# State space stage: decay operands of three groups in four as one VectorE product over four heads, of the fourth as four ScalarE activations

## The chip, the cores and the metric

The kernel runs on one core of a Trainium2 chip. The metric is device time in microseconds (us). Engines are named as in the profile: PE is TensorE (PEld its weight loads), DVE is VectorE, ACT is ScalarE, POOL is GpSimd, SP the engine that issues the DMAs.

## The reference, cut to what matters

Two layers of a hybrid block over 1024 latent tokens and 256 context tokens, model width 1024. Each layer has one input projection, three groups of heads side by side (neighbourhood attention, differential attention, a bidirectional state space model), an output projection, and a gated MLP with a convolution. The change touches one product in the state space part. With la = dt * a per token and head, and chunks of 128 tokens, the reference computes

```
cs = jnp.cumsum(la, axis=-1)
lmat = jnp.exp(jnp.where(lower, cs[..., :, None] - cs[..., None, :], -jnp.inf))
cb = jnp.einsum('bcign,bcjgn->bgcij', cm, bm)
y_diag = jnp.einsum('bgcij,bgecij,bcjgep->bcigep', cb, lmat, xdt)
```

for 8 heads in 2 groups of 4, once forwards and once backwards in time. All of it is float32.

## The kernel before, in words

The 1280 tokens are 10 chunks of 128: 8 of latents, 2 of context. Layer 0 produces all 10, layer 1 only the 8 of the latents, so there are 18 chunks in all.

In `ssd_out` the decay matrix of a group of four heads (`decay(g)`, lines 987 to 1004) comes from a matmul: a triangular 0/1 matrix `tri` times an operand `mf` of 128 partitions by 4 heads by 128 columns. `mf` holds, for each of four heads, a triangular 0/1 mask (`C(C_PI)` forwards, `C(C_SI)` backwards, 128x128 in SBUF) times a value per partition, `lah[:, e, c, h]`. `lah` holds la in two parts, e = 0 the rounded high part and e = 1 the rest. So a group needs four tiles `mf` (two directions, two parts), numbered i = 0 to 3 in the code, and four matmuls (line 998) that add up in one PSUM tile `pd` of the tag "s" (2 buffers). The tag "mf" has 3 buffers. ACT then takes the exponential into a tile `M` (line 1001, through the helper `act`, whose line is 93), and DVE multiplies it by the two masked score tiles `cbu` and `cbl` (line 1003). `out_pair(g)` uses `M` in the matmuls of line 1018.

Before the change, each `mf` is written by four products of 128x128, heads 0 and 2 on GpSimd, heads 1 and 3 on VectorE (line 996). This makes 18 chunks x 2 groups x 4 tiles = 144 tiles, and 576 products, half on each engine.

`ssd_all` steps the chunks as a generator. It runs in the background of the projections of the same layer: `dfproj` (differential q, k and v) and `naqk` (neighbourhood q and k). After each projection chunk `bg_step` advances the generator at 1.2 steps (`SR`). A projection chunk is 24 matmuls into a PSUM tile of the tag "mm" (3 buffers) and then an evacuation: square on ACT, a matmul for the mean, four activations on ACT and two or three products on DVE (`rstd`, lines 406 to 414), the scaling on DVE (lines 493 and 690), for differential q and k a rotation with one product on GpSimd (line 497), and a split into two parts (lines 281 and 282, or 697 and 698 with the rest on GpSimd). In the same chunk loop GpSimd also writes `xd` (964), `yo` (985) and `y` (1048) of the state space part and `wL` (269), the low part of the next projection weights.

The program is written as a data flow; a planner orders the instructions of each engine from estimated times, and adds the semaphores. Each engine then works through its own list in order, so an instruction that waits holds all behind it on its engine. GpSimd and ACT issue no DMAs here; all are issued on SP.

Of the kernel before, what the change touches and what calls it, by code (L numbers as in the profile page):

```python
# [12 lines left out]
ACTF = mybir.ActivationFunctionType  # L13
ALU = mybir.AluOpType
# [66 lines left out]
def hybrid_kernel(ctx, tc, xin, cc, w_ada, bada, gmf, w_in, w_dt, w_out, w_up, w_dn, vec, cst, rope, nab, out):  # L81
    nc = tc.nc
    V, S, G, PE, SP = nc.vector, nc.scalar, nc.gpsimd, nc.tensor, nc.sync
# [8 lines left out]
    def act(**kw):  # L92
        ins = S.activation(**kw)  # L93
        f = kw["func"]
        if f == ACTF.Silu:
            last_silu[0] = ins
            if last_exp[0] is not None:
                tc.add_manual_dep(ins.ins, last_exp[0].ins.name, nosync, reason="table")
        elif f in (ACTF.Exp, ACTF.Ln) and anchor[0] is not None:
            tc.add_manual_dep(ins.ins, anchor[0].ins.name, nosync, reason="table")  # L100
            cur_exp[0] = ins
        return ins
# [77 lines left out]
    def C(off, n=128, p=128):  # L180
        return cs[0:p, off:off + n]
# [93 lines left out]
    def pst(tag, bufs):  # L275
        if mmx[0] is None:
            tag, bufs = "B", 4
        return psx[1].tile([128, 512], F32, tag=tag, name=tag, bufs=bufs)
# [664 lines left out]
    def ssd_out(l, p, c, dts, lah, ecs):  # L943
        def v4(a):
            return a.rearrange("p (h d) -> p h d", h=4)
# [24 lines left out]
        for nm, mk in (("cbu", C_PI), ("cbl", C_SI)):  # L970
            t = p.tile([128, 2, 128], F32, tag=nm, name=nm, bufs=1)
            V.tensor_tensor(out=t, in0=pcb[:, 0:256].rearrange("p (g i) -> p g i", g=2),
                            in1=C(mk).unsqueeze(1).to_broadcast([128, 2, 128]), op=ALU.mult)
# [14 lines left out]
        def decay(g):  # L988
            pd = pst("s", 2)
            i = 0  # L990
            for d, mk in ((0, C_PI), (1, C_SI)):
                for e in range(2):
                    mf = p.tile([128, 4, 128], F32R, tag="mf", name="mf", bufs=3)
                    for hh in range(4):
                        h = 8 * d + 4 * g + hh
                        (V if hh % 2 else G).tensor_scalar(out=mf[:, hh], in0=C(mk), scalar1=lah[:, e, c, h:h + 1], scalar2=1.0,  # L996
                                        op0=ALU.mult, op1=ALU.mult)
                    PE.matmul(pd, tri[:, d], mf.rearrange("p h i -> p (h i)"), start=(i == 0), stop=(i == 3))  # L998
                    i += 1
            mm_ = p.tile([128, 2, 4, 128], F32, tag="M", name="M", bufs=2)  # L1000
            act(out=mm_[:, 1], in_=v4(pd), func=ACTF.Exp)
            for d in range(2):
                V.tensor_tensor(out=mm_[:, d], in0=mm_[:, 1],
                                in1=cbm[d][:, g].unsqueeze(1).to_broadcast([128, 4, 128]), op=ALU.mult)
            Ms[g] = mm_
# [3 lines left out]
        def out_pair(g):  # L1009
            if g == 0:  # L1010
                py[0] = pst("o", 1)
            for q in (2 * g, 2 * g + 1):
                PE.matmul(py[0][:, q * 128:(q + 1) * 128], offs[0][:, q * 128:(q + 1) * 128], ident,
                          start=True, stop=False)
                for d in range(2):
                    for e in range(2):
                        h = 2 * q + e
                        PE.matmul(py[0][64 * e:64 * e + 64, q * 128:(q + 1) * 128], xd[d][:, h * 64:(h + 1) * 64],
                                  Ms[g][:, d, h % 4], start=False, stop=(d == 1))

        decay(0)
        yield
        decay(1)
        yield
        out_pair(0)
# [6 lines left out]
        for q in range(4):  # L1032
            V.scalar_tensor_tensor(out=y[:, q], in0=ux[:, q], scalar=vcol(l, V_DSK + q),
                                   in1=py[:, q * 128:(q + 1) * 128], op0=ALU.mult, op1=ALU.add)
# [8 lines left out]
        for q in range(4):  # L1043
            V.scalar_tensor_tensor(out=y[:, q], in0=y[:, q], scalar=vcol(l, V_SN + q), in1=rs,
                                   op0=ALU.mult, op1=ALU.mult)
# [836 lines left out]
```

## Time and profile before

| | |
|---|---|
| median of 3 timed runs | 3596.09 us (3594.19 to 3603.89) |
| the profiled execution, own time | 3589.41 us |
| its span, first to last instruction | 3587.6 us |
| mean granted clock of TensorE | 0.965 |
| busy: PE, PEld | 3284.6 us (92%), 2582.9 us (72%) |
| busy: DVE, ACT, POOL | 2350.0 us (66%), 1515.8 us (42%), 1766.9 us (49%) |

Busy times are sums over the whole span, and matmul ends are modelled, so a busy PE isn't PE at its peak. The state space output runs twice: from about 310 to 580 us (layer 0) and from about 2215 to 2430 us (layer 1). These are the stretches that the views below are asked for. In a row of grouped instructions, "128x512 fp32r<-128x128 f32" gives the shapes written and read, "x160" the count, then the busy time in us, the mean of one in ns, and behind the second bar the idle time of the engine just before them with what ended it.

### The profile page before, as it was taken

The page shows a single profiled execution, that of the slowest core. Times are in us where ns is not written, and L with a number is a line of the kernel's source. Part 1 is how long each engine was busy: PE and PEld are TensorE (multiplying, and loading weights), DVE is VectorE, ACT ScalarE, POOL GpSimd, SP SyncE. Part 2 cuts the span into 40 slices and gives each one's busy share as a digit, 9 for nine tenths or more (in the row PEclk, how much of TensorE's full clock was granted, in tenths as well). Part 3 has the DMA queues.
Part 4 walks back from the last instruction along what each step waited for, and adds up shares of the span by engine and source line. Part 5 has one row for each costly group of instructions (what it writes and reads, how often), then busy time and mean ns, then how long its engine had stood idle before and what let it go on. Part 6 is the DMA issues. An engine that isn't in the chain of part 4 may idle for free. (4 is left out here: it accounts for less than half of the span.)

```text
span 3587.6 us, 50299 instructions
## 1 busy us (share of the span) xinstructions
PE 3284.6 (92%) x17970; PEld 2582.9 (72%) x17970; DVE 2350.0 (66%) x4208; ACT 1515.8 (42%) x2641; POOL 1766.9 (49%) x1319
## 2 busy tenths in 40 slices
PE   6998998899897999999998998998999969999899
PEld 3876776666676888887787776776666757777677
DVE  6635876778475655556858754985884576676763
ACT  4233434677353233233335523344774443333343
POOL 2136663656335444444554226763664445555444
PEclk8999999999998999999999999998999989999999
DMA  8255444753731222225443246446655522223643
GB/s 294 102 195 172 130 127 137 188 150 98 248 110 62 93 73 85 95 85 183 144 137 104 81 135 206 133 124 176 184 151 181 184 68 84 96 91 97 235 121 120
DMA packets 328474, 491.24 MB, mean 137 GB/s; under 512 B 28320, under 2 KB 182048, under 8 KB 327968
## 3 DMA queue, kind: packets, MB, share of 16 engines
q1 hardware_dynamic: 328224, 488.03, 42.6%
q8 instruction: 142, 2.33, 0.3%
q14 instruction: 108, 0.88, 0.1%
HBM read 349.25 MB, written 138.67 MB: 136 GB/s over the span
## 5 line engine op out<-in xcount | busy, mean ns | idle before, releaser
L269 POOL TENSOR_TENSOR wL<-wr,wH 128x1024 fp32r<-128x1024 f32 x80 | 203.8, 2551 | 417.1 <-ACT wH L268 389.5
L1227 POOL TENSOR_TENSOR wL<-wr,wH 128x1024 fp32r<-128x1024 f32 (+1 forms) x102 | 228.6, 2243 | 339.0 <-ACT wH L1224 304.4
L1227 POOL TENSOR_TENSOR wL<-wd,wH 128x512 fp32r<-128x512 f32 (+1 forms) x134 | 214.0, 1616 | 206.0 <-ACT wH L1224 201.4
L1227 POOL TENSOR_TENSOR wL<-ws,wH 128x512 fp32r<-128x512 f32 x168 | 253.4, 1528 | 112.0 <-ACT wH L1224 111.9
L758 DVE TENSOR_SCALAR_CACHE_REDUCE e<-s 128x512 f32<-128x512 f32 (+1 forms) x400 | 228.7, 588 | 105.5 <-PE s L757 101.0
L1227 DVE TENSOR_TENSOR bL<-br,bH 128x512 fp32r<-128x512 f32 x154 | 144.8, 943 | 133.9 <-ACT bH L1224 133.0
L93 ACT ACTIVATE e<-e,nm 128x1280 f32<-128x1280 f32 (+1 forms) x144 | 183.0, 1271 | 52.4 <-DVE nm L761 47.5
L757 PE MATMUL s<-ks,qst 128*128 128x512 f32 (+1 forms) x400 | 165.3, 450 | 39.5 <-DVE e L758 25.7
L1224 ACT CAST wH<-wr 128x1024 fp32r<-128x1024 f32 (+1 forms) x102 | 91.8, 905 | 252.4 <-PE mm L1219 188.2
L1224 ACT CAST wH<-ws 128x512 fp32r<-128x512 f32 x168 | 98.0, 619 | 231.5 <-PE mm L1219 94.3
L776 POOL TENSOR_TENSOR e<-e 128x1280 f32<-128x1280 f32 (+1 forms) x72 | 192.9, 2679 | 3.9
L774 POOL TENSOR_SCALAR e<-e,rho 128x1280 f32<-128x1280 f32 (+1 forms) x72 | 89.6, 1245 | 179.4 <-DVE rho L766 77.1
L996 POOL TENSOR_SCALAR mf<-cs,lah 128x128 fp32r<-128x128 f32 x288 | 141.3, 507 | 48.1 <-PE s L998 46.3
L1374 DVE SCALAR_TENSOR_TENSOR fa<-fpad,vc,fa 128x1282 f32<-128x1282 f32 (+1 forms) x88 | 140.6, 1653 | 36.7 <-ACT fa L93 36.7
L1224 ACT CAST bH<-br 128x512 fp32r<-128x512 f32 x154 | 95.3, 620 | 137.8 <-DMA br<-hdd 67.4
L1219 PE MATMUL A<-bL,wH 128*128 128x512 f32 x352 | 141.7, 403 | 11.9 <-DVE bL L1227 11.7
L1224 ACT CAST wH<-wd 128x512 fp32r<-128x512 f32 (+1 forms) x134 | 86.7, 682 | 136.0 <-PE B L1219 70.9
L422 PE MATMUL mm<-h_0H,wH 128*128 128x512 f32 x320 | 134.1, 420 | 4.4 <-DVE aqs L690 3.1
L1220 PE MATMUL A<-bH,wL 128*128 128x512 f32 x352 | 138.0, 398 | 0.0
L757 PEld LDWEIGHTS s<-ks,qst 128*128 128x128 f32 x400 | 75.4, 201 | 84.9 <-DVE e L758 52.6
L422 PE MATMUL mm<-h_1H,wH 128*128 128x512 f32 x320 | 132.2, 414 | 1.5 <-ACT z L93 1.5
L423 PE MATMUL mm<-h_0L,wH 128*128 128x512 f32 x320 | 131.1, 410 | 2.3 <-DVE h_0L L402 2.3
(871 smaller groups left out, 10812.8 us busy)
## 6 DMA issues: line engine op xcount, KB each, us to landing
wr<-in_w_up_dram SPq DMA_DIRECT2D x94, 512.0 KB
br<-hdd SPq DMA_DIRECT2D x154, 256.0 KB
wa<-in_w_ada_dram SPq DMA_DIRECT2D x56, 512.0 KB
wr<-in_w_in_dram SPq DMA_DIRECT2D x48, 512.0 KB
hdd<-c SPq DMA_DIRECT2D x88, 256.0 KB
wr<-in_w_ada_dram SPq DMA_DIRECT2D x40, 512.0 KB
wd<-in_w_dn_dram SPq DMA_DIRECT2D x38, 512.0 KB
hdd<-fa SPq DMA_DIRECT2D x66, 256.0 KB
```

What stands on the lines that cost most here:

```text
L93: ins = S.activation(**kw)
L269: (eng or G).tensor_tensor(out=wl, in0=wr, in1=wh.bitcast(F32), op=ALU.subtract)
L422: PE.matmul(ps[:, :n], wh[:, ks], r, start=(i == 0), stop=False)
L757: PE.matmul(s_, qst[b, qt][:, mi], ks[b][:, mi, k0 + c:k0 + c + n], start=True, stop=True)
L758: V.tensor_scalar(out=e[:, c:c + n], in0=s_, scalar1=1.0, scalar2=None, op0=ALU.mult, op1=ALU.max, accum_out=mx[:, ci:ci + 1])
L776: G.tensor_tensor(out=es[0][:, 0:nk], in0=es[0][:, 0:nk], in1=es[1][:, 0:nk], op=ALU.add)
L996: (V if hh % 2 else G).tensor_scalar(out=mf[:, hh], in0=C(mk), scalar1=lah[:, e, c, h:h + 1], scalar2=1.0, op0=ALU.mult, op1=ALU.mult)
L1219: PE.matmul(ps, wh, bl, start=False, stop=False, skip_group_check=True)
L1220: PE.matmul(ps, wl, bh, start=False, stop=last, skip_group_check=True)
L1224: S.copy(out=out_h, in_=src)
L1227: le.tensor_tensor(out=out_l, in0=src, in1=out_h.bitcast(F32), op=ALU.subtract)
L1374: V.scalar_tensor_tensor(out=a[:, :W], in0=pads[r][:, j:j + W], scalar=vcol(l, fw + j), in1=a[:, :W], op0=ALU.mult, op1=ALU.add)
```

## The change

In `decay(g)`, the four products of a tile become one VectorE product over 128 x 4 x 128 for i = 0, 1, 2: the mask is broadcast over the heads and the four values per partition over the columns. For i = 3 (backwards, low part) they become four ScalarE activations of function Identity with the value as the scale. GpSimd writes no part of `mf` any more. Tiles, buffers, matmuls and all else stay.

```
                     mf = p.tile([128, 4, 128], F32R, tag="mf", name="mf", bufs=3)
-                    for hh in range(4):
-                        h = 8 * d + 4 * g + hh
-                        (V if hh % 2 else G).tensor_scalar(out=mf[:, hh], in0=C(mk), scalar1=lah[:, e, c, h:h + 1], scalar2=1.0,
-                                        op0=ALU.mult, op1=ALU.mult)
+                    h0 = 8 * d + 4 * g
+                    if i == 3:
+                        for hh in range(4):
+                            act(out=mf[:, hh], in_=C(mk), func=ACTF.Identity, scale=lah[:, e, c, h0 + hh:h0 + hh + 1])
+                    else:
+                        V.tensor_tensor(out=mf, in0=C(mk).unsqueeze(1).to_broadcast([128, 4, 128]),
+                                        in1=lah[:, e, c, h0:h0 + 4].unsqueeze(2).to_broadcast([128, 4, 128]), op=ALU.mult)
                     PE.matmul(pd, tri[:, d], mf.rearrange("p h i -> p (h i)"), start=(i == 0), stop=(i == 3))
```

## Rows read from the trace of the kernel before

**Rows 1.** Busy time of each engine in the two stretches, with granted clock

```profile
310.00:580.00 270.00, 247.34 (x1428) 188.77 (x1426) 221.38 (x455) 105.52 (x211) 168.84 (x223) 0.97 0.42 130
2215.00:2430.00 215.00, 203.32 (x1152) 155.51 (x1150) 175.51 (x351) 85.56 (x166) 147.38 (x188) 0.96 0.46 143
sum 485.00, PE 450.66 PEld 344.28 DVE 396.89 ACT 191.07 POOL 316.22; mean PE 225.33 PEld 172.14 DVE 198.44 ACT 95.54 POOL 158.11
```

**Rows 2.** Waits of PE in 310 to 580: us in total, times, longest

```profile
PE s L1040 <- DVE yrs L1039: 3.1, 4, 1.5
PE s L998 <- DVE mf L996: 3.1, 2, 1.9
PE mm L422 <- DVE aqs L690: 3.1, 2, 2.9
PE mm L422 <- DVE qn L493: 2.1, 1, 2.1
PE o L1018 <- DVE M L1003: 1.9, 2, 1.7
PE s L998 <- POOL mf L996: 1.1, 3, 0.6
```

**Rows 3.** The same view, 2215 to 2430

```profile
PE t L496 <- DVE qn L493: 6.4, 2, 5.9
PE o L1018 <- DVE M L1003: 2.2, 1, 2.2
PE o L1013 <- POOL yo L985: 1.0, 2, 0.7
PE s L998 <- POOL mf L996: 0.9, 3, 0.4
```

**Rows 4.** Tile mf: min/median/max ns; and "who waited for it (us, times)"

```profile
L996 POOL TENSOR_SCALAR mf<-cs,lah x288: 363/442/1316, 310.9 to 2423.1; 128x128 fp32r<-128x128 f32 x144
L996 DVE TENSOR_SCALAR mf<-cs,lah x288: 267/314/2430, 313.8 to 2423.1; 128x128 fp32r<-128x128 f32 x144
...
  POOL mf L996: 47.9, 32
  DVE mf L996: 18.0, 16
```

**Rows 5.** Busy time of the instructions on tile mf alone: PE, PEld, DVE, POOL

```profile
sum 485.00, PE 52.40 PEld 25.63 DVE 110.86 POOL 141.33; mean PE 26.20 PEld 12.81 DVE 55.43 POOL 70.67
```

**Rows 6.** Line 1003, a DVE product of 512 columns from two SBUF tiles, all 72

```profile
L1003 DVE TENSOR_TENSOR M<-M,cbu x36: 675/700/2517, 335.9 to 2427.7; 128x512 f32<-128x512 f32 x36
L1003 DVE TENSOR_TENSOR M<-M,cbl x36: 674/692/2776, 339.1 to 2428.9; 128x512 f32<-128x512 f32 x36
```

**Rows 7.** The same products grouped, 310 to 580

```profile
L1003 DVE TENSOR_TENSOR M<-M,cbu 128x512 f32<-128x512 f32 x20 | 17.7, 885 | 3.4 <-ACT M L93 3.3
L1003 DVE TENSOR_TENSOR M<-M,cbl 128x512 f32<-128x512 f32 x20 | 16.8, 838 | 0.3
```

**Rows 8.** The same, 2215 to 2430

```profile
L1003 DVE TENSOR_TENSOR M<-M,cbl 128x512 f32<-128x512 f32 x16 | 15.5, 967 | 0.2
L1003 DVE TENSOR_TENSOR M<-M,cbu 128x512 f32<-128x512 f32 x16 | 13.3, 829 | 0.8 <-ACT M L93 0.7
```

**Rows 9.** In order of time: four DVE products in a row, eight on POOL

```profile
439.86 0.93 DVE L996 TENSOR_SCALAR mf<-cs,lah 128x128 fp32r<-128x128 f32 x4
...
374.61 4.06 POOL L996 TENSOR_SCALAR mf<-cs,lah 128x128 fp32r<-128x128 f32 x8
```

**Rows 10.** ACT, activations of 128x128 in 310 to 580

```profile
L93 ACT ACTIVATE yrv<-s,epst 128x128 f32<-128x128 f32 x9 | 3.2, 361 | 1.2 <-PE s L1040 1.1
L93 ACT ACTIVATE yrs<-yrs 128x128 f32<-128x128 f32 x9 | 2.8, 307 | 0.1
```

**Rows 11.** Waits of ACT in 310 to 580

```profile
ACT qoh L93 <- PE t L491: 31.3, 10, 9.5
ACT zt L93 <- DVE y L1035: 16.5, 7, 5.4
ACT dfv L511 <- PE mm L448: 12.8, 6, 4.6
```

## The prediction

> **What bounds the kernel now.** I read the busy table by stage first, over the two stretches in which the state space output runs [rows 1]. PE is busy 450.7 of 485 us, so it sets the pace, with 34.3 us of idle time. DVE is next: 396.9 us, 82% of the time. POOL has 316.2 us (65%) and ACT 191.1 us (39%). The reader should see that two engines are nearly full in the same stretch. PE's idle time can't be waste alone, because an 82% busy DVE that works in order is late whenever its work comes in bunches. The granted clock is 0.97 and 0.96, so PE lost another 0.03 x 270 + 0.04 x 215 = 16.7 us of full-speed work there. Idle time and lost clock, 51 us, are the most that anything done here can give back.
>
> Next I asked what ended PE's waits [rows 2, 3]. Those that a DVE or POOL result ended add up to 14.4 us in layer 0 and 10.5 us in layer 1, 24.9 us together. Of these 3.1 + 1.1 + 0.9 = 5.1 us are for the decay operand itself (DVE once, POOL twice); the other 19.8 us are for other results of the two engines (the projection's scaling, M, the norm).
>
> Then the tile mf [rows 4, 5]. Its 576 products keep DVE busy for 110.9 us and POOL for 141.3 us of the two stretches: more than a quarter of all DVE work there, and 45% of POOL's. The writers also wait for one of the three buffers to be read by its matmul: POOL 47.9 us in 32 waits, DVE 18.0 us in 16. Waiting means that all behind them on the same engine waits too.
>
> **The change part by part.** Removed on POOL: 288 products, 141.3 us [rows 5], and the buffer waits of 47.9 us. POOL falls from 316 to 175 us. Nothing of it was PE's bound directly except the 2.0 us of POOL mf waits [rows 2, 3], but eight of these products take 4.06 us in a row [rows 9], and they were the slower half of every tile.
>
> Removed on DVE: 288 products of 128 columns, 110.9 us, a mean of 385 ns where four in a row take 0.93 us, 233 ns each [rows 5, 9]. So DVE paid more than half as much again as the operation costs undisturbed, while both engines worked on the same tile.
>
> Added on DVE: 108 products of 512 columns. The trace has no product with both operands broadcast; the nearest row is line 1003, also 512 columns, two SBUF inputs, one of them broadcast. It takes 675 ns at least and 700 in the median [rows 6], and 829 to 967 ns in the mean [rows 7, 8]; over all 72, 63.3 us / 72 = 879 ns. Bounds for the 108: 108 x 0.675 = 72.9 us and 108 x 0.967 = 104.4 us, so DVE saves between 38 and 6 us. The mean lies over the median because a few take up to 2.8 us; POOL was 65% busy while they ran, and will be 36% busy. I take 0.79 us, half-way between median and mean: 85.3 us, a saving of 25.6 us. The same relief should reach the other DVE products with two SBUF inputs. For line 1003 the excess over 0.69 us is 63.3 - 49.7 = 13.6 us; I take half of it, 7 us, and nothing for the other lines (bounds 0 and 13.6). DVE: 396.9 - 25.6 - 7 = 364 us, 75% in place of 82%.
>
> One rule speaks against this edit. The trace has the old product at 233 ns per 128 columns and the nearest new one at 700 ns per 512, so one long product is cheaper than four short ones by 0.23 us [rows 6, 9]. The Trainium skill, "VectorE: DVE Perf Modes", section "The perf-mode tier table", says that float32 tensor_scalar reaches twice the rate and tensor_tensor only the single rate: per column the new form is the slower one. By that rate alone 512 columns would take 2 x 0.93 = 1.86 us, and the 108 products 201 us instead of 85; the median of 700 ns does not agree with reading the rule so, since most of a short product is a fixed cost, and the row decides.
>
> Added on ACT: 36 tiles x 4 = 144 activations of 128x128. Rows for this size are 307 ns (SBUF input) and 361 ns (PSUM input, a bias tile) [rows 10]; a scale read per partition isn't among those with 128 columns, so I take the range: 44 to 52 us, 48 us in the middle. ACT rises from 191 to 239 us of 485, 49%. Identity is used in the same stretches already, so no new function. What hides it: ACT mostly waits for others. In layer 0 it waits 31.3 us for the mean's matmul, 12.8 us for the value projection and 16.5 us for a DVE product [rows 11]. So its own work costs nothing as long as it is free when the projection's evacuation arrives.
>
> Moved to ACT with it: the buffer wait. With three buffers, the tile i = 3 takes the buffer of i = 0 of the same group and must wait for that tile's matmul. Today such a wait costs POOL 47.9 / 32 = 1.5 us and DVE 1.1 us. On ACT, the exponential of the group before and the activations of the projection's evacuation are queued behind it; DVE's scaling (lines 493 and 690) waits for those, and PE's next projection chunk waits for the PSUM tile. Bounds: nothing, if the order puts the four activations behind the matmul, or 36 x 1.5 = 54 us of held ACT. I take nothing net on PE, since ACT waits for PE more than PE for ACT; both ends stay in the range. The DMA issues aren't touched: no DMA is issued on ACT or POOL, and SP passes nothing.
>
> The sum. For the operand itself: the last product of a group of four tiles no longer comes from a POOL run of 4 us but from three DVE products (3 x 0.7 = 2.1 us) beside 4 x 0.33 = 1.3 us on ACT. Of 5.1 us I expect 1 to be left: -4. For the other 19.8 us: how late a nearly full engine is goes roughly with busy / idle, 0.82 / 0.18 = 4.5 before and 0.75 / 0.25 = 3.0 after, a third less: -6.6. For the clock: it fell around PE's pauses, so I take the same third of 16.7: -5.6. Together -16 us. Against the profiled execution (3589.4 us, of which 1.8 us lie outside the span) this gives 3573 us; the median of the timed runs is 6.7 us above that execution, so the forecast on the median is 3596 - 16 = 3580 us.
>
> **The rivals.**
>
> A: PE takes nothing of it. PE is 93% busy in the stretches, and what DVE no longer delays is delayed by something else: a transfer, a PSUM tile, ACT. For: 34.3 us idle are only partly ended by DVE and POOL. Against: 24.9 of them are. What is left then is the direct operand waits, at most -5: 3591 us.
>
> B: slower, by ACT as the new place of the wait. Mechanism: the four activations of i = 3 stand ahead of an evacuation in ACT's list and wait for the matmul of i = 0. Price: 36 waits x 1.5 us = 54 us, against the 16 us of the forecast. It is slower by more than 0.3% (11 us) from the point where 27 of the 54 us, half, reach PE; with three quarters, 40 us, it comes to 3596 + 24 = 3620 us. For: the buffer waits are in the trace now, 48 in number, and ACT's chain of four activations per projection chunk is one that PE's PSUM tiles depend on. Against: ACT is half idle, and the three "mm" tiles give slack of more than one chunk.
>
> C: the new products are as slow as line 1003 at its worst, 967 ns, for POOL's remaining work still runs beside them. DVE then saves 6 us, not 33, and stays at 81%; the direct waits go (-4), the rest hardly: 3590 us. The Trainium skill, "SBUF — State Buffer", section "Who interferes with whom", gives a reason: a DVE instruction with two SBUF inputs and a GpSimd one that reads SBUF exclude each other. The maxima of 2.5 to 2.8 us on line 1003 agree with it.
>
> D: the planner, whose order rests on estimated times, reorders the stretches so that the change does not do what its counts say; the time can move to either side by what the waits of rows 2 and 3 are worth, 10 to 20 us.
>
> **How the numbers follow.** Forecast 3580 us: 0.50, its own range 3560 to 3586. A and C together: 0.24, 3586 to 3596. B: 0.14, 3607 to 3632. D: 0.12, both sides alike. About 0.3%, 11 us, is what a measurement of this kernel can tell from no change: faster is below 3585, slower above 3607. Faster: nearly all of the forecast, a little of A and C, half of D: 0.60. Slower: B and a quarter of D: 0.17. The same: 0.23. If all of the 24.9 us of waits and 16.7 us of clock came back it would be 3554 us; so the range goes from 3556, and up to 3607, where it leaves out most of B.
>
> **What would show it.** Right: in the two stretches DVE busy near 364 us and POOL near 175 us, the new products at 0.70 to 0.85 us, ACT near 239 us, no PE wait of over 1 us for mf, PE idle down by 10 us, and the stretches shorter by some 16 us. Wrong: ACT waiting for the matmul of line 998 with more than 20 us in total and PE's projection matmuls waiting for ACT (B); the products at 0.95 us (C); PE idle unchanged, with other names on it (A); a change of more than 5 us outside the two stretches (D).

## The result: slower by 0.76%

The changed kernel takes 3623.18 us in the median of 4 runs (3621.36 to 3627.36), the kernel before 3595.91 us beside it (3594.19 to 3603.89). The ratio is 1.0076, 95% interval 1.0058 to 1.0095, or +27 us. The forecast was 3580 us with a range up to 3607, so both the side and the range were wrong. The profiled execution took 3621.36 us, span 3619.6, mean clock 0.961.

The first view answers to [rows 1]: busy time by engine (PE, PEld, DVE, ACT, POOL) in the two stretches of the changed kernel, then granted clock, DMA share and GB/s.

```profile
311.00:588.00 277.00, 250.78 (x1418) 190.81 (x1417) 214.23 (x349) 128.52 (x291) 92.08 (x63) 0.93 0.41 126
2227.00:2453.00 226.00, 206.75 (x1164) 156.97 (x1164) 175.43 (x278) 104.74 (x231) 92.51 (x60) 0.95 0.45 137
sum 503.00, PE 457.53 PEld 347.78 DVE 389.66 ACT 233.26 POOL 184.59; mean PE 228.77 PEld 173.89 DVE 194.83 ACT 116.63 POOL 92.29
```

The stretches are 18 us longer, 503 in place of 485. PE idles 45.5 us in place of 34.3, and the clock in layer 0 fell from 0.97 to 0.93. Over the whole span the mean clock of 0.961 in place of 0.965 is 3619.6 x 0.039 - 3587.6 x 0.035 = 15.6 us of full-speed work, half of the 32 us between the two spans. The engines got nearly what was forecast (POOL 185 us for 175, ACT 233 for 239), but DVE fell only by 7 us in the stretches, not by 33.

The tile mf, as in [rows 4], and its busy time, as in [rows 5]:

```profile
L93 ACT ACTIVATE mf<-cs,lah x144: 384/388/406, 334.3 to 2430.3; 128x128 fp32r<-128x128 f32 x144
L999 DVE TENSOR_TENSOR mf<-cs,lah x108: 673/685/2835, 315.1 to 2428.6; 128x512 fp32r<-128x512 f32 x108
...
  DVE mf L999: 27.5, 23
  ACT M L93: 23.1, 13
  ACT mf L93: 22.5, 13
...
sum 503.00, PE 52.44 PEld 26.00 DVE 88.40 ACT 46.10; mean PE 26.22 PEld 13.00 DVE 44.20 ACT 23.05
```

A product has a median of 685 ns and a mean of 88.40 / 108 = 819 ns (I took 790). The 144 activations take 46.1 us (I gave 44 to 52). The waits for a buffer are there on both engines: 27.5 us on DVE, 22.5 us on ACT.

PE's waits of the changed kernel, first layer 0, answering to [rows 2], then behind the dots layer 1, [rows 3]; us in total, times, longest:

```profile
PE s L968 <- DMA ux<-ud: 6.7, 1, 6.7
PE s L1043 <- DVE yrs L1042: 5.2, 1, 5.2
PE o L1021 <- DVE M L1006: 4.3, 4, 2.1
...
PE t L496 <- DVE qn L493: 6.2, 2, 5.9
PE s L1043 <- DVE yrs L1042: 5.1, 2, 3.7
PE o L1021 <- DVE M L1006: 3.5, 3, 3.0
PE s L1001 <- DVE mf L999: 2.4, 2, 2.0
```

The waits for the operand fell from 5.1 to 2.4 us, as the forecast wanted, and other waits grew: for `yrs`, for `M`, and for the DMA of `ux`, which before was the longest wait of layer 0 already, 4.0 us (the view of [rows 2] has it above the lines shown there).

To see where the time goes, I compared the start of the same projection matmul in both traces (one execution of each). The changed kernel lags by 1.6 us near 330, 11.9 near 390, 7.2 at 580, 11.7 at 2190, 11.4 at 2360, 24.2 at 2420, 32.0 at 2790 and 31.8 at 3580. So it loses about 10 us between 360 and 390, 12 us between 2360 and 2420, and 8 us in the attention behind layer 1's stretch. The place near 380 on PE: before (start, us, the instruction, then idle time before it with its releaser)

```profile
377.55 0.46 PE L1040 MATMUL s<-yrs,cs 128*128 128x128 f32 x2 [1.47 <-DVE yrs L1039]
377.77 0.71 PE L998 MATMUL s<-mf,tri 128*128 128x512 f32 x2
378.72 0.50 PE L998 MATMUL s<-mf,tri 128*128 128x512 f32 x1 [0.25 <-POOL mf L996]
379.06 0.60 PE L968 MATMUL s<-ux 128*128 128x128 f32 x4
379.50 1.02 PE L496 MATMUL t<-qn,cs 128*128 128x512 f32 x2
```

and changed:

```profile
380.37 0.50 PE L1001 MATMUL s<-mf,tri 128*128 128x512 f32 x1
386.07 0.79 PE L1043 MATMUL s<-yrs,cs 128*128 128x128 f32 x2 [5.19 <-DVE yrs L1042]
386.51 1.63 PE L1001 MATMUL s<-mf,tri 128*128 128x512 f32 x3
387.94 1.91 PE L496 MATMUL t<-qn,cs 128*128 128x512 f32 x2
```

Two things are to be seen. PE stood 5.19 us for `yrs`, and its matmuls then ran at the lower clock level (the pair on "qn" 1.91 us in place of 1.02). And the list itself is another one: the four matmuls on `ux` no longer stand between the decay matmuls and the pair on "qn". DVE and POOL at that place, before (first DVE, then POOL):

```profile
376.38 1.02 DVE L1039 TENSOR_REDUCE yrs<-zt 128x128 f32<-128x512 f32 x1
...
379.09 2.45 DVE L1003 TENSOR_TENSOR M<-M,cbu 128x512 f32<-128x512 f32 x1
```

```profile
378.64 2.35 POOL L269 TENSOR_TENSOR wL<-wr,wH 128x1024 fp32r<-128x1024 f32 x1
```

and changed:

```profile
380.44 3.44 DVE L999 TENSOR_TENSOR mf<-cs,lah 128x512 fp32r<-128x512 f32 x2
383.80 0.68 DVE L414 SCALAR_TENSOR_TENSOR qrs<-qoh,qrs 128x512 f32<-128x512 f32 x1
384.40 0.68 DVE L999 TENSOR_TENSOR mf<-cs,lah 128x512 fp32r<-128x512 f32 x1
385.01 1.01 DVE L1042 TENSOR_REDUCE yrs<-zt 128x128 f32<-128x512 f32 x1
```

```profile
379.93 2.79 POOL L269 TENSOR_TENSOR wL<-wr,wH 128x1024 fp32r<-128x1024 f32 x1
```

Two products took 3.44 us instead of 1.3 while POOL wrote `wL` for 2.79 us, and three stand ahead of the `yrs` that PE waits for. Before, `yrs` was done when `wL` began, and it was a product on `M` that took 2.45 us beside it. The Trainium skill, "SBUF — State Buffer", section "Who interferes with whom", says that a DVE instruction with two SBUF inputs contends with a GpSimd one that reads SBUF; this row agrees.

Next come the lists of the built programs, without the writers of mf. All engines have the same instructions in them, but 4548 of the 15,841 places in PE's list hold another matmul, and 1306 of 3320, 763 of 2412 and 148 of 1027 places in the lists of DVE, ACT and POOL another instruction. On PE all but ten of these places lie between about 325 and 935 us and between 2245 and 2770 us of the trace before: the state space stretches and the attention behind them. So two causes were possible: the operations, or the order. The experiments separate them.

### The profile page after: what moved, and what is told of

Read it like the earlier page. It is cut to its first block, busy times and chain, and to the rows that moved or that the text cites. A ratio compares the mean times of both kernels' runs of the same rounds, so it can differ in the third digit from the quotient of the medians.

```text
span 3619.6 us, 49915 instructions
## 1 busy us (share of the span) xinstructions
PE 3295.8 (91%) x17970; PEld 2591.3 (72%) x17970; DVE 2355.0 (65%) x4028; ACT 1558.8 (43%) x2785; POOL 1636.9 (45%) x1031
## 5 line engine op out<-in xcount | busy, mean ns | idle before, releaser
L1230 POOL TENSOR_TENSOR wL<-wr,wH 128x1024 fp32r<-128x1024 f32 (+1 forms) x102 | 228.8, 2245 | 340.8 <-ACT wH L1227 316.7
L424 PE MATMUL mm<-h_0H,wL 128*128 128x512 f32 x320 | 130.5, 408 | 0.0
```

The costliest lines, as they stand in the source:

```text
L1230: le.tensor_tensor(out=out_l, in0=src, in1=out_h.bitcast(F32), op=ALU.subtract)
```

## The experiments

**Parts of the change, in the planner's own order.** Products alone, the fourth tile as before:

```
                     if i == 3:
                         for hh in range(4):
-                            act(out=mf[:, hh], in_=C(mk), func=ACTF.Identity, scale=...)
+                            (V if hh % 2 else G).tensor_scalar(out=mf[:, hh], ...)
```

> The products of i = 0 to 2 as in the change, the tile i = 3 as before (two products on DVE, two on GpSimd). Theory 1 (the loss of 27 us is ACT holding its list while it waits for the buffer of the fourth tile, 22.5 us of such waits): no loss, 3580 to 3600 us. Theory 2 (the long products on DVE are the cost: they exclude GpSimd's long operations, one took 2.8 us): the loss stays, 3615 to 3630 us. Theory 3 (the planner's new order of PE's list, whatever the operations cost): anything within 3580 to 3630, not tied to the counts.

Measured 3625.89 us, ratio 1.0073 (1.0046 to 1.0101): as slow as the whole change, without any activation.

The activations alone, with the i < 3 branch as before:

```
                     else:
-                        V.tensor_tensor(out=mf, ...)
+                        for hh in range(4):
+                            (V if hh % 2 else G).tensor_scalar(out=mf[:, hh], ...)
```

> Only the fourth tile goes to ACT, the tiles i = 0 to 2 stay split between DVE and GpSimd. Theory 1 (ACT): the loss stays, 3615 to 3630 us. Theory 2 (products): no loss, 3585 to 3600 us. Theory 3 (order): anything within 3580 to 3630.

Measured 3598.41 us, 0.9997 (0.9982 to 1.0012). So the activations, the mechanism of rival B, are not what makes it slow. Nor does a new order cost time just by being new: PE's list of this kernel differs from that of before in 4260 places, nearly as many as the changed kernel's, at no cost.

All four tiles as products:

```
-                    if i == 3:
...
-                    else:
-                        V.tensor_tensor(out=mf, ...)
+                    V.tensor_tensor(out=mf, ...)
```

> All four tiles as DVE products, 144 in all, nothing on ACT or GpSimd. Theory 1 (ACT): 3580 to 3600 us, the loss is gone. Theory 2 (products): a third more of them, 3625 to 3640 us. Theory 3 (order): anything within 3580 to 3640.

Measured 3611.38 us, 1.0032 (1.0019 to 1.0046): more work on DVE than in the first of the three (2381.1 us busy in the whole span for 2348.4), and yet faster. That doesn't fit a cause in DVE's load alone.

The kernel before with its heads exchanged between the engines, meant to disturb only the order:

```
-                        (V if hh % 2 else G).tensor_scalar(out=mf[:, hh], ...)
+                        (G if hh % 2 else V).tensor_scalar(out=mf[:, hh], ...)
```

> The kernel before with the two engines exchanged: heads 0 and 2 on DVE, 1 and 3 on GpSimd. The same operations in the same number on each engine. Theories 1 and 2: no difference, 3590 to 3602 us. Theory 3 (order): the planner makes another list of the same work, and the time moves by 5 us or more.

Measured 3599.74 us, 1.0001 (0.9986 to 1.0017). The planner's order came out the same as before, so this says nothing of order.

**Operations and order crossed.** An engine's instructions are logged as they are emitted (all but the writers of mf and the two-part reductions). At the end each is tied to the one ahead of it in the order of the other kernel, without a semaphore, so that only the planner's choice is bound. The held lists agree place by place with the order held to. Either kernel held to its own order builds to the same program as without the edit, instruction for instruction and wait for wait, so the added ties cost nothing by themselves. The writers of mf are not held: the planner chooses their place.

```
+    V0, S0, G0 = V, S, G
+    V, S, G, PE = Logged(V, logs["V"]), Logged(S, logs["S"]), Logged(G, logs["G"]), Logged(PE, logs["PE"])
...
+    for e, text in ORDER.items():
+        seq, log = unpack(text), logs[e]
+        for a, b in zip(seq, seq[1:]):
+            tc.add_manual_dep(log[b].ins, log[a].ins.name, nosync, reason="order")
```

The changed operations under the old order:

> The changed operations, with PE, DVE, ACT and GpSimd held to the order that the planner made for the kernel before (every instruction but the writers of mf, whose place the planner chooses). Order theory: the operations are as cheap as forecast and the loss came from the new order, so the loss is gone: 3575 to 3598 us. Operations theory (long products on DVE, activations on ACT cost it): still 3615 to 3630 us.

Measured 3598.58 us, 1.0012 (0.9996 to 1.0029). The loss is gone, and nothing of the forecast gain is there: the half of the order theory that held the operations to be as cheap as forecast missed.

The operations of before under the new order (the same edit on the kernel before, with the other list):

> The operations of the kernel before (half on DVE, half on GpSimd), with the four engines held to the order that the planner made for the changed kernel. Order theory: as slow as the change or slower, 3615 to 3640 us. Operations theory: 3590 to 3602 us, as before.

Measured 3619.24 us, 1.0075 (1.0049 to 1.0101). The order alone is as slow as the change. With PE's list alone held (the "V", "S" and "G" lists left out), first the change, then the kernel before:

```
-    "V": [...], "S": [...], "G": [...],
```

> The changed operations with PE alone held to the old order; the planner orders the rest around it. If the order of PE's list is what matters: like the run with four engines held, 3575 to 3598 us. If the order of DVE and ACT matters: 3600 to 3630. Operations theory: 3615 to 3630 us.

> The operations before with PE alone held to the new order. If the order of PE's list is what matters: 3615 to 3640 us. Operations theory: 3590 to 3602 us.

Measured 3600.16 us, 1.0016 (1.0000 to 1.0033), and 3616.34 us, 1.0059 (1.0038 to 1.0080). The first lies 2 us over its range, the second in it. The other engines then nearly follow by themselves (126 of 3320 places in DVE's list differ in the first). Four kernels at one place, 360 to 425, columns as in the first view: before, changed, changed with the old order, before with the new order.

```profile
360.00:425.00 65.00, 57.95 (x321) 42.54 (x320) 55.69 (x112) 29.43 (x56) 39.57 (x49) 0.95 0.41 127
```

```profile
360.00:425.00 65.00, 55.10 (x286) 39.50 (x284) 50.95 (x84) 30.24 (x69) 20.93 (x13) 0.88 0.37 114
```

```profile
360.00:425.00 65.00, 57.89 (x352) 43.23 (x351) 54.47 (x95) 33.29 (x72) 29.57 (x17) 1.00 0.44 138
```

```profile
360.00:425.00 65.00, 57.44 (x287) 39.38 (x286) 51.75 (x112) 24.34 (x47) 36.38 (x50) 0.87 0.40 122
```

The clock and the matmuls done go with the order (321 and 352 at 0.95 and 1.00; 286 and 287 at 0.88 and 0.87), not with the operations. The windows are the same stretch of time, not of work, in one execution each.

The changed operations with the old order in one layer only, the list being cut between the layers, first in layer 0, then in layer 1 (the two edits are shown in short: OLD and NEW stand for the lists of the two kernels):

```
-ORDER = OLD
+ORDER = OLD[:cut] + NEW[cut:]
```

> The changed operations, four engines held to the old order up to the end of layer 0's attention and to the new order in layer 1. If the new order costs in both layers, as the traces suggest (some 10 us in layer 0, 20 in layer 1): 3608 to 3620 us, most of the loss. If layer 0's order is the cause alone: 3590 to 3602 us.

```
-ORDER = OLD
+ORDER = NEW[:cut] + OLD[cut:]
```

> The changed operations, the new order in layer 0 and the old order in layer 1. If both layers cost: 3600 to 3612 us. If layer 1's order is the cause alone: 3590 to 3600 us. If the two add up, this loss and that of the other half make the whole loss of 27 us.

Measured 3610.09 us, 1.0038 (1.0019 to 1.0057), and 3608.22 us, 1.0039 (1.0022 to 1.0057). The layer whose order is new costs about the same in both, some 0.26% over the 1.0012 of none; no single place makes the loss. At 360 to 425 they say the same as the four kernels: 342 matmuls at 0.95 with layer 0's old order, 284 at 0.86 with its new one.

**Under one order: what the operations cost.** All from here hold the order of before. The first two repeat parts of the change:

```
                         for hh in range(4):
-                            S0.activation(out=mf[:, hh], ...)
+                            (V0 if hh % 2 else G0).tensor_scalar(out=mf[:, hh], ...)
```

> The old order, the DVE products for i = 0 to 2, the tile i = 3 as before on DVE and GpSimd: no activation on ACT. If the activations ate the gain of the products: faster than the changed operations under the old order (3598.6), 3580 to 3594 us. If the products themselves are worth nothing under a fixed order: 3594 to 3606 us.

```
                     else:
-                        V0.tensor_tensor(out=mf, ...)
+                        for hh in range(4):
+                            (V0 if hh % 2 else G0).tensor_scalar(out=mf[:, hh], ...)
```

> The old order, only the tile i = 3 on ACT, the others split as before. If ACT's 46 us cost time: 3598 to 3612 us. If ACT hides them and the relief of DVE (28 us) counts: 3578 to 3592 us. If neither counts: 3592 to 3600 us.

Measured 3610.95 us, 1.0049 (1.0028 to 1.0070), and 3598.24 us, 0.9997 (0.9987 to 1.0007). The first is slower than either expectation allowed: without the activations, with 72 short products back on DVE, it takes 18 us more than the kernel before and 13 more than the changed operations. The second says that neither counts.

All four tiles as products (the third diff above, on V0), and each product issued twice:

> All four tiles as DVE products (144, nothing on ACT), under the old order. Order theory: no loss, 3590 to 3602 us, where the same operations in their own order took 3611 us. Operations theory: 3608 to 3620 us again.

```
+                        for _ in range(2):
                             V0.tensor_tensor(out=mf, ...)
```

> The changed operations under the old order, with each of the 108 DVE products issued twice into the same tile (the second repeats the first): 108 x 0.7 = 76 us more work for DVE in the two stretches. If the load of DVE sets the time, as the forecast assumed (a third of PE's DVE waits for 33 us of DVE): 3615 to 3650 us. If PE's fixed list sets it and DVE has slack between its deadlines: 3598 to 3610 us.

Measured 3614.21 us, 1.0057 (1.0038 to 1.0076), and 3641.70 us, 1.0139 (1.0108 to 1.0169). Here operations do cost time under the old order: the first is as the operations theory has it, the second as the load of DVE has it. Both give DVE more work than the change does. Each activation twice:

```
+                            for _ in range(2):
                                 S0.activation(out=mf[:, hh], ...)
```

> The changed operations under the old order with each activation for mf issued twice: 46 us more on ACT. If ACT's load costs in this stretch: 3608 to 3625 us, so that the first 46 us cost about as much. If ACT hides it, as the forecast said: 3594 to 3603 us.

Measured 3616.15 us, 1.0054 (1.0035 to 1.0073), 15 us above the kernel with one set. PE's waits, with the activations once and twice, 300 to 600 and behind the dots 2200 to 2480 (held kernels show the logging helper's line, 96, for most instructions):

```profile
PE s L96 <- ACT mf L1163: 1.8, 1, 1.8
...
PE s L96 <- ACT mf L1163: 1.3, 2, 0.9
```

```profile
PE s L96 <- ACT mf L1164: 9.3, 5, 3.6
...
PE s L96 <- ACT mf L1164: 8.6, 5, 3.1
```

The direct waits for ACT rise from 3.1 to 17.9 us, about the whole of the 15 us. So ACT's second set is on the path where the first hardly was.

A candidate for a better kernel, the operations of before with the fourth tile wholly on GpSimd:

```
-                        (V0 if hh % 2 else G0).tensor_scalar(...)
+                        (V0 if hh % 2 and i < 3 else G0).tensor_scalar(...)
```

> The kernel before under its own order, with the tile i = 3 written by four GpSimd products in place of two and two: 72 short products off DVE (72 x 0.233 = 17 us of its undisturbed work), 72 more on GpSimd (some 35 us), ACT untouched. If DVE's own undisturbed work on mf sets the time under a fixed order (about 0.7 us per us): 3582 to 3590 us, faster than both kernels. If GpSimd's longer run for the fourth tile holds the matmul: 3598 to 3610 us.

Measured 3603.71 us, 1.0006 (0.9993 to 1.0020): 72 short products less on DVE, and no gain. It lies where the expectation put GpSimd's longer run: PE's waits for mf from POOL are 4.0 + 3.1 = 7.1 us in the two stretches, in place of 2.0.

Last, is anything to be had here? One kernel writes no operand at all, one leaves out the fourth alone (`fixed` is written once per layer):

```
-                    mf = p.tile([128, 4, 128], F32R, tag="mf", name="mf", bufs=3)
...
+                    mf = fixed
```

> Leaves out all writing of the decay operands: the 144 matmuls read one tile that is written once per layer, and no engine writes mf (the result is not the reference's). The order of TensorE, VectorE, ScalarE and GpSimd is held to that of the kernel before. It takes 111 us of VectorE and 141 us of GpSimd out of the two stretches, and every wait for an operand or for an operand's buffer. Theory 'some time is to be had, and the change only failed to get it': the waits of TensorE for mf (5 us) and part of the other 19.8 us that VectorE and GpSimd end go, 3574 to 3586 us, ratio 0.994 to 0.997. Rival 'TensorE takes nothing of it under this order': within 0.2% of the kernel before, 3589 to 3603 us; then no division of the operand's work among the engines could have gained anything here.

```
                     if i == 3:
-                        for hh in range(4):
-                            S0.activation(out=mf[:, hh], ...)
+                        mf = fixed
```

> The changed operations without the four activations: the operand of i = 3 is not computed, its matmul reads the tile that is written once per layer (the result is not the reference's). Three products on VectorE as in the change, order held to that of the kernel before. The same with the activations took 3598.6 us, ratio 1.0012; with each activation twice 1.0054, so 46 us more of ScalarE cost 15 us. Theory 'ScalarE's time is on the path': taking the first 46 us away gives the same back, 3580 to 3587 us, ratio 0.996 to 0.998. Rival 'there was slack for the first set and not for the second': 3594 to 3600 us, ratio 0.999 to 1.0015.

Measured 3568.34 us, 0.9933 (0.9920 to 0.9946), and 3591.77 us, 0.9999 (0.9988 to 1.0009). The first theory holds of the first, and a little more than it asked: all of the operand's work is worth 24 us under this order (19 to 29 by the interval). The rival holds of the second, by the ratio: the first set of activations had slack for nearly all of its time. In the first, DVE falls by 78.5 us against [rows 1] and the clock rises to 0.99:

```profile
310.00:580.00 270.00, 254.49 (x1547) 200.56 (x1546) 176.07 (x310) 110.85 (x225) 95.55 (x66) 0.99 0.47 143
2200.00:2415.00 215.00, 202.58 (x1185) 156.47 (x1184) 142.29 (x238) 86.00 (x166) 86.50 (x61) 0.97 0.46 144
sum 485.00, PE 457.06 PEld 357.03 DVE 318.36 ACT 196.85 POOL 182.04; mean PE 228.53 PEld 178.51 DVE 159.18 ACT 98.42 POOL 91.02
```

## Why the prediction was wrong, step by step

**The step that failed: the lists were taken to stay as they are.** The sum priced every operation in the order of before. The trace can't show the order of a kernel that isn't built, but the section on the kernel before says that a planner orders it from estimated times. Rival D named this, sized at 10 to 20 us either side with a chance of 0.12. Of the 43 us between forecast and result, 23 to 25 stand here. The crossed runs:

| ratio to before | old order | new order |
|---|---|---|
| operations of before | 1 | 1.0075 |
| changed operations | 1.0012 | 1.0076 |

The order is worth 0.64% under the changed operations (23 us) and 0.75% under the old ones (27 us); the operations 0.12%, not told from nothing. PE's list alone carries 0.59 of the 0.75%.

**The second step: the relief of DVE was read from busy time.** This would have made the forecast wrong under the old order too, where the change gained nothing; the other 19 us or so of the 43 stand here. I set 110.9 us of short products [rows 5] against 85.3 us of long ones, a saving of 25.6. On the tile itself most of it came: 88.4 us in the changed kernel and 93.0 with the old order, 22.5 and 17.9 less. But over the whole span DVE is busy 2355.0 and 2343.3 us in these two, in place of 2350.0. So it got +5.0 and -6.7 us, not -33: the rest of its work took 27.5 and 11.2 us longer.

```profile
PE 3279.9 (91%) x17970; PEld 2578.5 (72%) x17970; DVE 2343.3 (65%) x4028; ACT 1556.9 (43%) x2785; POOL 1645.5 (46%) x1031
```

This is section 1 of the page with the old order. Busy time holds the time in which an instruction is held up beside POOL (3.44 us for two products, 2.45 us for one, in the rows near 380), and as I read it the next instruction takes over the hold-up when one goes; no run shows that step by itself. Undisturbed, four short ones take 0.93 us [rows 9], 0.233 each, and long ones follow at 0.605 us, here in the changed kernel:

```profile
388.36 0.69 DVE L1006 TENSOR_TENSOR M<-M,cbl 128x512 f32<-128x512 f32 x1
388.96 0.69 DVE L999 TENSOR_TENSOR mf<-cs,lah 128x512 fp32r<-128x512 f32 x1
389.57 0.28 DVE L410 SCALAR_TENSOR_TENSOR yrv<-zt,yrv 128x128 f32<-128x128 f32 x1
```

By these spacings it is an estimate of 288 x 0.233 = 67.1 us before and 108 x 0.605 = 65.3 us after: the change takes almost nothing from DVE's own work. The runs under one order stand so, with the busy time of DVE over the whole span as the pages have it:

| operand's work under the old order | DVE on mf, us undisturbed (estimate) | DVE busy, whole span, against before, us | others | time against before, us |
|---|---|---|---|---|
| none | 0 | -79.7 | | -24 |
| before, fourth tile on GpSimd | 50.3 | -10.2 | POOL more | +2 |
| fourth tile on ACT, rest as before | 50.3 | -19.5 | ACT 46 us, POOL less | -1 |
| three products, fourth left out | 65.3 | -13.6 | no POOL | 0 |
| the changed operations | 65.3 | -6.7 | ACT 46 us, no POOL | +4 |
| before | 67.1 | 0 | POOL half | 0 |
| the change, activations twice | 65.3 | -7.5 | ACT 91 us | +19 |
| three products, fourth as before | 82.1 | +10.0 | POOL less | +18 |
| four products | 87.1 | +15.4 | no POOL | +20 |
| the change, products twice | 130.7 | +66.7 | ACT 43 us | +50 |

The last column is ratio minus one, times 3596 us; the third is one execution each. Both measures of DVE put the runs in nearly the same order, and the time follows them, all but the doubled activations, where PE's waits account for the loss. Between 50 and 67 us of undisturbed work hardly anything moves, above it the time climbs, and only taking away everything gives time back. The busy time of the tile alone doesn't do it: three products with the fourth as before have 106.6 us and lose 18 us, the kernel before has 110.9 us. With nothing written, 110.9 us of busy time went and DVE fell by 79.7, nearer to the 67.1. The table orders the runs but shows no mechanism.

**Relief of the other DVE products (-7 us): didn't come.** The 40 products on `M` in layer 0 took (17.7 + 16.8) / 40 = 862 ns before [rows 7] and 905 ns after, though POOL was busy 92.1 us there in place of 168.8; in layer 1 the mean went from 900 [rows 8] to 969 ns. In layer 0:

```profile
L1006 DVE TENSOR_TENSOR M<-M,cbu 128x512 f32<-128x512 f32 x20 | 21.4, 1069 | 1.8 <-ACT M L93 1.8
L1006 DVE TENSOR_TENSOR M<-M,cbl 128x512 f32<-128x512 f32 x20 | 14.8, 739 | 0.2
```

**The third less of other waits (-6.6) and of lost clock (-5.6): wrong as a rule.** With the old order and the changed operations, DVE is 78% busy in the stretches in place of 82% (310 to 580, and 2208 to 2423 where its layer 1 lies), and PE idles 485 - 448.5 = 36.5 us, not less than the 34.3 of before:

```profile
sum 485.00, PE 448.47 PEld 343.81 DVE 378.38 ACT 232.53 POOL 191.89; mean PE 224.23 PEld 171.90 DVE 189.19 ACT 116.27 POOL 95.94
```

The lost clock, reckoned as in the forecast, is 0.07 x 277 + 0.05 x 226 = 30.7 us in the changed kernel in place of 16.7: the term put at -5.6 came as +14.

**The operand's own waits (-4): half right.** 5.1 us became 2.4 in the changed kernel, 4.4 with the old order. ("DVE once, POOL twice" in the prediction counts rows; they hold two waits and six.)

**The rivals.** A, that PE takes nothing of it, is what happens under a fixed order. B had the right side and the wrong cause: ACT did hold its list for mf (22.5 us), but the activations cost nothing that can be told against leaving the fourth tile out (1.0012 and 0.9999, intervals that overlap). C has the price wrong, 967 ns for the measured 819, and one consequence right: it let DVE save 6 us in the stretches, and it saved 7 (the time that C put to it, 3590 us, is not the one measured). D was the case, larger than sized, and with the sign named for it: the span grew by 32 us and the stretches by 18, so 14 us lie outside them. But D gave no side, and the prediction had no reason for the slow one.

**Still open:** why the planner's order for the new estimates is the worse one. Its own order against the old one cost +0.64% for the change and +0.24% for the products alone, nothing for the activations alone, and gained 0.25% for four products; the intervals of the second and the last pair overlap. That isn't tied to any count that I found, and not to the number of moved matmuls: 4548, 4498, 4260 and 4663 places of PE's list in these four. The order's loss is 10 us near 380 and 20 us in layer 1 in the traces; why just these matmuls moved was not tried.

## What to carry to other kernels

Where a planner orders the program, a local edit changes two things, so build the crossed pair (new operations in the old order, old operations in the new one) before explaining a time by the operations. Price removed work at its undisturbed spacing, not at its busy time, which holds what neighbours add. And leave the work out wholly once: that shows the most that another division of it could give under one order, here 24 us, of which none of the divisions tried reached any.

## What the runs showed of the hardware

- A 5.19 us pause of PE is followed by matmuls at the lower of the two clock levels, half speed: granted clock 0.53 from 381 to 392 in the changed kernel, 1.00 from 377 to 388 before, and the pair on "qn" took 1.91 us in place of 1.02. So this wait cost more than its own length.

```profile
381.00:392.00 11.00, 5.93 (x11) 3.46 (x12) 10.45 (x16) 3.59 (x11) 2.99 (x2) 0.53 0.22 76
```

```profile
377.00:388.00 11.00, 10.20 (x48) 7.23 (x48) 10.96 (x22) 4.60 (x10) 8.95 (x13) 1.00 0.16 50
```

- A half-idle engine had slack for one set of work and not for two: 46 us more on ACT, 48% busy then, cost nothing that can be told the first time (1.0012 against 0.9999, some 5 us) and 15 us the second.
- Busy time doesn't all leave with the work that showed it: with the order of before and no operand written, 110.9 us of DVE's busy time went, and DVE's whole busy time fell by 79.7 us (2350.0 to 2270.3).
